# Hybrid decoder layer on one core: short products alternated with long ones in a planned order, and norm weights that ride with x

## The chip, the cores and the metric

The kernel runs on one core of a Trainium2 chip. The metric is the device time of one execution in microseconds. Five engines carry it: TensorE (PE; its weight loads are listed apart, as PEld), VectorE (DVE), ScalarE (ACT), GpSimd (POOL), and SyncE (SP), which here only starts DMAs.

## What is computed

One layer of a decoder for 512 tokens of width 1024, all in fp32. Cut to what matters here:

```
h = rmsnorm(x, norm_mix_g)
c_q, c_kv, k_r, u_ssm, x_q, gate_logits = split(h @ w_in)
y_a = mla_branch(...) @ w_o_mla        # 8 heads, causal attention in blocks of 128
y_b = s5_branch(u_ssm, ...) @ w_o_ssm  # 32 groups, state 64, complex diagonal scan, GLU
y_c = cross_branch(x_q, mem, ...) @ w_o_cross  # 4 heads over 256 memory tokens
x = x + (sum_i sigmoid(gate_i) * y_i) @ w_out
up = causal_dwconv(rmsnorm(x, norm_ffn_g) @ w_up, conv_w, conv_b)   # width 3, 2 x 2816 columns
x = x + (silu(up_g) * up_v) @ w_down
```

In the S5 branch the coefficients of the state space model are worked out on the chip from lambda, dt, B and C. The cross branch multiplies the normed memory by w_mem_kv (1024 x 1024).

## The kernel before

**Products.** Every large fp32 product is three products of a faster type (fp32r). `split` (L456) makes a high part of an operand on ACT and the rest, the low part, by a subtraction on DVE or POOL; `mm3` (L489) multiplies high by high, high by low and low by high into the same PSUM bank. The stationary operand of a product is at most 128 columns, the moving one mostly 512. Weights come in units of 128 x 1024: `wload` (L471) starts the DMA on SP into one of two slots "wr", `wsplit` (L479) makes the two parts in one of three slots "ws". A unit of w_in or w_out feeds 24 products of 512 columns. A unit of w_mem_kv feeds 12 (two chunks of the contraction, two token tiles, three products).

**Short products.** Beside the long ones PE runs transposes (128 x 128, results in `pstr`), products with 128 moving columns (in `pssc`), the statistics (stationary `accx` or `am`, moving a single column `ones`), and, for the state space model, products of 32 and 96 columns with stationary `pad` tiles that have 32 columns (shown as `128*32`).

**What sets the order.** `trace` (L413) runs the kernel once as a draft, in which each instruction becomes an Op. The text ORDER (L54) has one letter for each step of a generator: h is `gen_xstats`, m `gen_mem`, a `gen_stage_a`, s, p, t and e the state space model, and so on; the last stages, `w_out_ffn` (L1312), come behind all of them. `order_ops` (L263) then lists the Ops for five engines at once: it takes the Op that could start first by a table of costs (`_lengths`, L159), adds a lag (LAG) before other engines may use a result, lets some Ops choose between DVE, ACT and POOL, and does so twice, the second time with urgencies from the first. The engines' instructions are issued in that order by one line, L1464, so that every row of the profile has this line and is told by its tiles. On each engine the order is fixed: an instruction that waits holds back all behind it on its engine.

**The start.** Eleven matmuls on a zero tile (`wz`) run while the first DMAs are under way. For each of the eight chunks of x, SP starts the chunk `xc` and its weights `wu`; behind the first chunk SP also starts a small DMA for `pg`, the norm weights of x, and POOL's queue one for `pv`, all other per-column parameters. ACT and DVE make `xs` (high and low) from `xc` and `pg`, and 12 products for each chunk give the input of the state space model. `acc` (`accx` in rows) collects the squares of x.

**The statistics.** `gen_xstats` (L562) sums `accx` over partitions by eight products with one moving column. Four of them read a contiguous stationary block of 128 columns, four every fourth column (`acc[:, t::4]`). DVE copies the sums to `mx`, POOL raises them to the power -0.5, four transposes of `mx` spread the result over partitions, and a copy to `rB` on DVE ends it. Meanwhile and after that DVE works through the state space coefficients: small operations on `ang`, `ap`, `den`, `pw`, then wide ones on `Bp`, `bt` and `G`, between the low parts of weight units.

**The end.** The down projection makes eight tiles of the output. The last one (m = 7) is made in two halves of 256 columns, 66 products each, each with its own add on DVE and its DMA on SP.

Of the kernel before, what the change touches and what calls it, by code (L numbers as in the profile page):

```python
# [18 lines left out]
KC = D // 128  # L19
# [19 lines left out]
def _split_bits(v, bits):  # L39
# [15 lines left out]
    "aZmsemhha1pupakpp1pttktmt2utpt11ppxpepxtupxtttctp1cxxuttYtatkd1taxggdxgg1dcxaccrdBcccdddBd1qdBBdqdqq2dvvvwvwCq"  # L55
    "vwvq2wqvv00v2wCvwwvwvwvwvvwwqww0w2q2wwvqwwwvqvvv0wwvvvq0qw2wqwCv0wvvvww0wvwwwvwvwvwww0v2wwwCAAAA"
# [7 lines left out]
PSUM_TAGS = ("mm", "sc", "tr")  # L64
LAG = {"PE": 2000.0, "V": 600.0, "S": 600.0, "P": 600.0, "SP": 60.0}
# [8 lines left out]
class Op:  # L74
    __slots__ = ("eng", "calls", "var", "idx", "touch", "deps", "succ", "nbytes", "tiles", "step", "acc")
# [61 lines left out]
def describe(op, tiles):  # L137
# [18 lines left out]
    op.acc = "PE" in op.calls  # L156


def _lengths(op, eng, nm, args, kw, outs, ins, tiles):  # L159
# [12 lines left out]
    if eng == "PE":  # L172
        st, mov = (ins[1], ins[0]) if nm == "transpose" else (ins[0], ins[1])
        if nm == "transpose":
            n, p = _free(st), _free(mov)
            ldw = p / 1.2 + 5
            return max(n / 2.4 + 2, ldw), 275.0, ldw, lock, func
        n, p = _free(mov), _free(st)
        ldw = (p / 1.2 + 5) * (2 if st.ap[-1][0] > 1 else 1)
        if mov.dtype == F32:  # L180
            half = max(n / 1.2 + 4, ldw)
            return 2 * half, n / 1.2 + half + 175, ldw, lock, func
        return max(13 + n / 2.4, ldw), n / 2.4 + 176, ldw, lock, func
# [79 lines left out]
def order_ops(ops, bufs, urgency=None):  # L263
# [23 lines left out]
    dma_free, dve_busy, pool_busy = 0.0, (0.0, 0.0), (0.0, 0.0)  # L287
# [41 lines left out]
    while done < len(ops):  # L329
        best = None  # L330
        for e in engs:
            a, pick, rk = avail[e], None, ranks[e]
            for i in cand[e]:
                op = ops[i]
                r = max(ready_at[i][e], a)
                if (best is not None and r >= best[0]) or (pick is not None and (r, rk[i]) > pick[:2]):
                    continue
# [34 lines left out]
        else:  # L372
# [40 lines left out]
def trace(alloc, V, S, P, T, SP, VP, VS, VSP, xT, memT, pos, freq, pv, grow, lam, sbc, dcol, wu, wa, wqb, wkvb, wglu, wxk, wxq, wmem,  # L413
# [84 lines left out]
    for _ in range(11):  # L498
# [3 lines left out]
    pvt, pg = cst([128, NPV], b="pv"), cst([128, KC], b="pg")  # L502
# [23 lines left out]
    ur = [k8([128, 4, L], b="wu") for _ in range(2)]  # L526
    for kc in range(KC):
        xcs.append(k2([128, L], b="xc"))
        SP.dma_start(xcs[kc], xT[:, kc])
        if kc == 0:  # L530

            SP.dma_start(pg, pv[:, PV["norm_mix_g"]:PV["norm_mix_g"] + KC])
            P.dma_start(pvt, pv)
        SP.dma_start(ur[kc // 4][:, kc % 4], wu[:, kc])
    for kc in range(KC):
# [776 lines left out]
    def w_out_ffn():  # L1312
# [58 lines left out]
        for m in range(KC):  # L1371
            p = ps("mm")
            halves = [slice(0, L)] if m < KC - 1 else [slice(0, 256), slice(256, L)]
# [115 lines left out]
def _layout(inp):  # L1489
# [5 lines left out]
    o["xT"] = _rows(np.ascontiguousarray(w["x"].T))  # L1495
    o["memT"] = _rows(np.ascontiguousarray(w["mem"].T))
# [66 lines left out]
```

## Time and profile before

| | before |
|---|---|
| time, median of 3 runs | 847.66 us (847.46 to 848.22) |
| profiled execution | 848.97 us |
| its span | 847.2 us |
| PE busy | 839.4 us, 4284 instructions |
| DVE busy | 593.2 us, 1092 instructions |
| ACT busy | 387.5 us, 658 instructions |
| POOL busy | 110.9 us, 118 instructions |
| DMA | 81.03 MB, mean 96 GB/s |

The span is what the hardware profiler records of one execution from the first to the last instruction. Starts and durations in rows are in us from the start of the span; an "x4" at a row's end joins four instructions in a row, and then the duration runs from the first start to the last end. Records of products overlap, since they are pipelined: the pitch of a product is the time from its start to the start of the next one.

### The profile page before, as it was taken

Reading aid. Unit: us, or ns where it says so; the run is one execution under the profiler, and the core shown is the slowest. Engines: PE = TensorE matmul, PEld = TensorE weight load, DVE = VectorE, ACT = ScalarE, POOL = GpSimd, SP = SyncE. Lnnn points to the kernel's source line nnn. Section 1 sums busy time; section 2 is a strip of 40 time slices with the busy share of each in tenths; the row PEclk is TensorE's granted clock in tenths of the full one; section 3 lists DMA queues with packets and bytes.
Section 4 is the critical chain, followed back from the end, with each engine's and each line's share of the span. In section 5 each row is a group of like instructions: output and inputs, shape, how many; then the busy total and the mean of one; then the engine's idle time right before and its main releaser. Section 6 shows DMA issues by size and latency. Waiting matters only on the chain.

```text
span 847.2 us, 11358 instructions
## 1 busy us (share of the span) xinstructions
PE 839.4 (99%) x4284; PEld 718.3 (85%) x4284; DVE 593.2 (70%) x1092; ACT 387.5 (46%) x658; POOL 110.9 (13%) x118
## 2 busy tenths in 40 slices
PE   9999999999999999999999999999999999999997
PEld 9878899998888888888888888888888888888887
DVE  7989998997677788768686539777777777423221
ACT  7746345547534575656444336444444444212110
POOL 5573141002112122120000002000000000000000
PEclk9899999999999999999999999999999999999999
DMA  9323322113123212321433323333333222333330
GB/s 320 118 77 98 117 64 75 51 59 104 44 72 88 88 40 69 118 75 51 149 124 100 100 75 99 100 100 100 99 100 97 91 90 90 118 111 106 119 100 26
DMA packets 26055, 81.03 MB, mean 96 GB/s; under 512 B 3104, under 2 KB 3664, under 8 KB 26000
## 3 DMA queue, kind: packets, MB, share of 16 engines
q1 hardware_dynamic: 25632, 79.45, 28.9%
q0 software_dynamic: 368, 0.85, 0.3%
q8 instruction: 34, 0.56, 0.3%
q14 instruction: 21, 0.17, 0.1%
HBM read 78.19 MB, written 2.10 MB: 95 GB/s over the span
## 4 chain that ended last, share of the span: by engine, by line
PE 93%; DVE 2%; DMA 2%; ACT 1%; issue 1%; POOL 1%; SPq 0%; DVEq 0%; POOLq 0%; ACTq 0%
PE psmm L1464 83%; PE pssc L1464 6%; PE pstr L1464 5%; DMA xc<-in_xT_dram 1%; DMA wr<-in_wg_dram 1%; POOL am L1464 0%; DVE ws L1464 0%; SPq L1464 0%; ACT ws L1464 0%; DVE ang L1464 0%; DVE ms L1464 0%; ACT xs L1464 0%; DVE am L1464 0%; DVE accx L1464 0%; POOL pad L1464 0%
## 5 line engine op out<-in xcount | busy, mean ns | idle before, releaser
L1464 ACT ACTIVATE ws<-wr 128x1024 fp32r<-128x1024 f32 (+3 forms) x140 | 142.7, 1021 | 322.0 <-PE psmm L1464 270.7
L1464 PE MATMUL psmm<-hs,ws 128*128 128x512 f32 x1008 | 229.4, 389 | 0.0
L1464 DVE TENSOR_TENSOR ws<-wr,ws 128x1024 fp32r<-128x1024 f32 x135 | 161.6, 1198 | 87.0 <-ACT ws L1464 86.6
L1464 PEld LDWEIGHTS psmm<-hs,ws 128*128 128x128 f32 x1008 | 189.0, 188 | 39.2
L1464 PE MATMUL psmm<-xs,ws 128*128 128x512 f32 x696 | 172.0, 396 | 0.0
L1464 PEld LDWEIGHTS psmm<-xs,ws 128*128 128x128 f32 x696 | 127.3, 188 | 25.2
L1464 PE MATMUL psmm<-act,ws 128*128 128x512 f32 (+1 forms) x594 | 120.7, 365 | 0.0
L1464 PEld LDWEIGHTS psmm<-act,ws 128*128 128x128 f32 x594 | 102.7, 189 | 18.1
L1464 DVE SCALAR_TENSOR_TENSOR cv<-z,pv,cv 128x511 f32<-128x511 f32 (+1 forms) x88 | 67.2, 770 | 1.0 <-ACT cv L1464 0.3
L1464 DVE TENSOR_TENSOR z<-psmm,r2B 128x512 f32<-128x512 f32 x42 | 29.0, 690 | 47.5 <-PE psmm L1464 47.5
L1464 PE MATMUL psmm<-mrg,ws 128*128 128x512 f32 x192 | 43.7, 389 | 0.0
L1464 PEld LDWEIGHTS psmm<-mrg,ws 128*128 128x128 f32 x192 | 36.0, 188 | 7.5
L1464 PE MATMUL psmm<-ws,xs 128*128 128x288 f32 (+2 forms) x240 | 39.8, 314 | 0.0
L1464 PEld LDWEIGHTS psmm<-ws,xs 128*128 128x128 f32 x240 | 36.9, 214 | 0.3
L1464 ACT ACTIVATE cv<-z,pv 128x512 f32<-128x512 f32 x44 | 35.0, 800 | 0.3 <-DVE z L1464 0.3
L1464 PE MATMUL psmm<-ws,ms 128*128 128x512 f32 x96 | 25.6, 426 | 0.0
L1464 DVE SCALAR_TENSOR_TENSOR gt<-gt,psmm 128x512 f32<-128x512 f32 x24 | 16.2, 683 | 12.9 <-PE psmm L1464 12.9
L1464 DVE TENSOR_TENSOR gt<-psmm,rB 128x512 f32<-128x512 f32 x24 | 16.3, 683 | 12.4 <-PE psmm L1464 12.1
L1464 PE MATMUL psmm<-xo,ws 128*128 128x512 f32 x96 | 24.7, 398 | 0.0
L1464 DVE TENSOR_TENSOR o<-psmm,x 128x512 f32<-128x512 f32 (+1 forms) x9 | 5.6, 631 | 26.3 <-PE psmm L1464 26.3
L1464 ACT ACTIVATE e<-pssc,nms,qsc 128x128 f32<-128x128 f32 (+3 forms) x32 | 19.6, 615 | 7.9 <-DVE nms L1464 7.6
L1464 PEld LDWEIGHTS psmm<-ws,ms 128*128 128x128 f32 x96 | 19.6, 209 | 4.3
(299 smaller groups left out, 1154.1 us busy)
## 6 DMA issues: line engine op xcount, KB each, us to landing
wr<-in_wup_dram SPq DMA_DIRECT2D x44, 512.0 KB, 3.5
wr<-in_wg_dram SPq DMA_DIRECT2D x24, 512.0 KB, 3.4
wr<-in_wdn_dram SPq DMA_DIRECT2D x16, 512.0 KB, 3.5
wr<-in_wmem_dram SPq DMA_DIRECT2D x8, 512.0 KB, 3.6
wr<-in_wout_dram SPq DMA_DIRECT2D x8, 512.0 KB, 3.5
wr<-in_wdn_dram SPq DMA_DIRECT2D x8, 384.0 KB, 3.0
wr<-in_wa_dram SPq DMA_DIRECT2D x5, 512.0 KB, 4.1
xc<-in_xT_dram SPq DMA_DIRECT2D x8, 256.0 KB, 6.3
```

What stands on the lines that cost most here:

```text
L1464: getattr(issue[ops[i].eng], name)(*args, **kw)
```

## The change

The scheduler, for products on PE: a product whose weight load is longer than its stream is now marked `short`. A transpose takes 35 ns of PE in the table instead of at least its weight load, and the other products are no longer held to at least their weight load. Instead a short product may only start `BETWEEN` = 225 ns or more after the last short one ended, so that the list puts long products between. ORDER is a new text of the same length. Then, in the program: the first chunk of x carries the eight columns of norm weights (input `xg`, tile `x0`), the DMA for `pg` is gone, and that for `pv` goes to SP behind the third chunk; the warm-up has 9 matmuls instead of 11; `gen_xstats` first copies `acc` with its columns rearranged to `accp`, so that the last four statistics read contiguous blocks; and the last output tile is made by 66 products of 512 columns, with its two adds as before and the second DMA on ACT's queue.

```diff
 ORDER = (
-    "aZmsemhha1pupakpp1pttktmt2utpt11ppxpepxtupxtttctp1cxxuttYtatkd1taxggdxgg1dcxaccrdBcccdddBd1qdBBdqdqq2dvvvwvwCq"
+    "Zesaphmhpeutmtppmtppp1ptu1xtx1aptp1xptu2kuttattpt1ttaxktcYxacxat1gkgcgxgdxc1drccd1BddccBdddBdqBqddq2vqvwvvvwww"
...
+BETWEEN = 225.0
...
+    op.short = op.acc and op.var["PE"][3] > 0
...
     if eng == "PE":
         st, mov = (ins[1], ins[0]) if nm == "transpose" else (ins[0], ins[1])
         if nm == "transpose":
-            n, p = _free(st), _free(mov)
-            ldw = p / 1.2 + 5
-            return max(n / 2.4 + 2, ldw), 275.0, ldw, lock, func
+            ldw = _free(mov) / 1.2 + 5
+            return 35.0, 275.0, ldw, max(ldw - 35.0, 0.0), func
...
-        return max(13 + n / 2.4, ldw), n / 2.4 + 176, ldw, lock, func
+        return 13 + n / 2.4, n / 2.4 + 176, ldw, max(ldw - 13 - n / 2.4, 0.0), func
...
                 r = max(ready_at[i][e], a)
+                if op.short:
+                    r = max(r, short_end + BETWEEN)
...
+            if op.short:
+                t = max(t, short_end + lock)
+                short_end = t + occ
...
-    for _ in range(11):
+    for _ in range(9):
         T.matmul(pz[:, :128], wz, wz, start=True, stop=True)
...
+    x0 = k8([128, L + KC], b="x0")
+    pg = x0[:, L:]
     for kc in range(KC):
-        xcs.append(k2([128, L], b="xc"))
-        SP.dma_start(xcs[kc], xT[:, kc])
-        if kc == 0:
-
-            SP.dma_start(pg, pv[:, PV["norm_mix_g"]:PV["norm_mix_g"] + KC])
-            P.dma_start(pvt, pv)
+        xcs.append(x0[:, :L] if kc == 0 else k2([128, L], b="xc"))
+        SP.dma_start(x0 if kc == 0 else xcs[kc], xg if kc == 0 else xT[:, kc])
         SP.dma_start(ur[kc // 4][:, kc % 4], wu[:, kc])
+        if kc == 2:
+            SP.dma_start(pvt, pv)
...
     def gen_xstats():
+        ap4 = k2([128, 4, 128], b="accp")
+        VS.tensor_copy(ap4, acc.rearrange("p (j t) -> p t j", t=4))
         pm = ps("tr")
         for t in range(4):
             T.matmul(pm[:, t:t + 1], acc[:, t * 128:(t + 1) * 128], ones, start=True, stop=True)
-            T.matmul(pm[:, 4 + t:5 + t], acc[:, t::4], ones, start=True, stop=True)
+        for t in range(4):
+            T.matmul(pm[:, 4 + t:5 + t], ap4[:, t], ones, start=True, stop=True)
...
-            halves = [slice(0, L)] if m < KC - 1 else [slice(0, 256), slice(256, L)]
...
-            for c in halves:
-                for k in range(NFF):
-                    u = un[k // 8]
-                    sl = slice((k % 8) * 128, (k % 8) * 128 + 128)
-                    mm3(p[:, c], u[:, 0, sl], u[:, 1, sl], act[0][k][:, c], act[1][k][:, c], k == 0, k == NFF - 1)
+            for k in range(NFF):
+                u = un[k // 8]
+                sl = slice((k % 8) * 128, (k % 8) * 128 + 128)
+                mm3(p, u[:, 0, sl], u[:, 1, sl], act[0][k], act[1][k], k == 0, k == NFF - 1)
...
-                SP.dma_start(outT[m, :, c], o[:, c])
+                (S if c.start else SP).dma_start(outT[m, :, c], o[:, c])
```

The order shows the rest. First PE at the first of four groups of products with `pad` (32 and 96 moving columns). Before, most of them run behind one another, here the last of the group:

```order
L1464 MATMUL pstr_250<-pad_152_234,pad_230 32x32
L1464 MATMUL pstr_250<-pad_153_235,pad_231 32x32
L1464 MATMUL pstr_250<-pad_232,pad_230 32x96
L1464 MATMUL pstr_250<-pad_233,pad_231 32x96
L1464 MATMUL psmm_258<-xs_90,ws_260 128x512
```

Now, the first of the same group:

```order
L1476 MATMUL psmm_252<-ws_261,ms_198 128x512
L1476 MATMUL pstr_244<-pad_103_185,pad_181 32x32
L1476 MATMUL psmm_253<-ws_261,ms_194 128x512
L1476 MATMUL pstr_244<-pad_104_186,pad_182 32x32
L1476 MATMUL pstr_244<-pad_183,pad_181 32x96
L1476 MATMUL psmm_253<-ws_261,ms_198 128x512
```

A product of 512 columns now stands between the two of 32 columns, and one behind that of 96; in the whole program the products with 32 stationary columns stand in 18 runs instead of 5. The other short products (transposes, and those with 128 columns), 476 in both programs, stand in 338 runs instead of 82.

The second place is PE at the first four transposes of `pad`. In `psmm`, products of `ws` with `ms` belong to a unit of w_mem_kv, products of `xs` with `ws` to a unit of w_in. Before, the units of w_mem_kv that stood behind the statistics were done by then, and two units of w_in were open:

```order
L1464 MATMUL psmm_222<-xs_97,ws_224 128x512
L1464 MATMUL psmm_226<-xs_90,ws_228 128x512
L1464 MATMUL psmm_226<-xs_98,ws_228 128x512
L1464 MATMUL psmm_242<-xs_90,ws_244 128x512
L1464 MATMUL psmm_242<-xs_98,ws_244 128x512
L1464 MATMUL pstr_240<-idt_88,pad_230 128x128 x4
L1464 MATMUL psmm_226<-xs_90,ws_228 128x512
```

Now (`ws_255`, `ws_257`, `ws_259` and `ws_261` are the last four of the eight units of w_mem_kv):

```order
L1476 MATMUL psmm_253<-ws_255,ms_195 128x512
L1476 MATMUL psmm_252<-ws_257,ms_192 128x512
L1476 MATMUL psmm_253<-ws_257,ms_192 128x512
L1476 MATMUL pstr_214<-idt_87,pad_181 128x128
L1476 MATMUL psmm_252<-ws_257,ms_192 128x512
L1476 MATMUL pstr_214<-idt_87,pad_181 128x128
L1476 MATMUL psmm_252<-ws_257,ms_196 128x512
L1476 MATMUL pstr_214<-idt_87,pad_181 128x128
L1476 MATMUL psmm_253<-ws_257,ms_192 128x512
```

All eight units of w_mem_kv, 12 products each, now follow the statistics at once. Before, only the four of the first half did, the fourth of them mixed with a unit of w_in, and then came units of w_in with 24 products each. From the statistics to the first use of the low part of `ws_261`, the last unit, PE now has 86 products of 512 columns, 16 transposes and three or four products of 128 columns, among them the rows shown here.

DVE over the same stretch. Before:

```order
L1464 TENSOR_TENSOR G_200<-bt_198,ap_168 128x1024
L1464 TENSOR_TENSOR ws_218<-wr_217,ws_218 128x1024
L1464 TENSOR_TENSOR ws_224<-wr_223,ws_224 128x1024
L1464 TENSOR_TENSOR Bp_199<-Bp_199,bt_198 128x16x16 x2
L1464 TENSOR_TENSOR G_200<-bt_198,ap_168 128x1024
```

Now:

```order
L1476 TENSOR_TENSOR ws_257<-wr_256,ws_257 128x1024
L1476 TENSOR_TENSOR ws_259<-wr_258,ws_259 128x1024
L1476 TENSOR_TENSOR Bp_162<-Bp_162,bt_161 128x16x48
L1476 TENSOR_TENSOR bt_161<-bt_161,ap_150 128x1024
L1476 TENSOR_TENSOR G_163<-bt_161,ap_150 128x1024
L1476 TENSOR_TENSOR G_163<-G_163,bt_161 128x1024
L1476 TENSOR_TENSOR bt_161<-bt_161,ap_150 128x1024
L1476 TENSOR_TENSOR ws_261<-wr_260,ws_261 128x1024
```

The same wide operations on Bp, bt and G are there, but nearly all of them stand between the statistics' `mx` and the low part of the last unit of w_mem_kv (`ws_261`), with the low parts of four other such units among them.

## Rows read from the trace of the kernel before

**Rows 1.** The page: busy time of the engines, and the chain of work that ended last, by engine.

```profile
PE 839.4 (99%) x4284; PEld 718.3 (85%) x4284; DVE 593.2 (70%) x1092; ACT 387.5 (46%) x658; POOL 110.9 (13%) x118
...
PE 93%; DVE 2%; DMA 2%; ACT 1%; issue 1%; POOL 1%; SPq 0%; DVEq 0%; POOLq 0%; ACTq 0%
```

**Rows 2.** What PE waited for in the whole span: us in total, times, the longest (two more rows, the last, have 1.0 us at the start and 0.4).

```profile
PE pstr L1464 <- POOL pad L1464: 1.9, 1, 1.9
```

**Rows 3.** Engines by stretch, the stretch right behind the statistics: us, then busy time of PE, PEld, DVE, ACT and POOL with instructions, the clock granted to PE as a share of full speed, DMA share and GB/s.

```profile
37.90:43.60 5.70, 5.70 (x15) 4.45 (x16) 2.97 (x19) 3.97 (x8) 1.65 (x1) 0.50 0.26 94
```

**Rows 4.** The timeline of PE around the statistics: start, duration, tiles.

```profile
34.03 1.43 PE L1464 MATMUL pstr<-ones,accx 128*128 128x1 f32 x8
...
37.90 6.99 PE L1464 MATMUL psmm<-ws,ms 128*128 128x512 f32 x18
44.72 0.60 PE L1464 MATMUL pstr<-idt,mx 128*128 128x128 f32 x4
```

**Rows 5.** The timeline of DVE behind the statistics: start, duration, tiles.

```profile
38.80 0.16 DVE L1464 TENSOR_SCALAR mx<-pstr 128x8 f32<-128x8 f32 x1
...
40.74 0.18 DVE L1464 TENSOR_TENSOR ap<-ang 128x16 f32<-128x16 f32 x1
45.36 0.69 DVE L1464 COPY rB<-pstr 128x512 f32<-128x512 f32 x1 [4.43 <-PE pstr L1464]
...
46.90 0.68 DVE L1464 TENSOR_TENSOR Bp<-bt,ang 128x512 f32<-128x512 f32 x1
...
48.10 1.21 DVE L1464 TENSOR_TENSOR G<-bt,ap 128x1024 f32<-128x1024 f32 x1
49.24 2.35 DVE L1464 TENSOR_TENSOR ws<-wr,ws 128x1024 fp32r<-128x1024 f32 x2
51.51 0.75 DVE L1464 TENSOR_TENSOR Bp<-Bp,bt 128x256 f32<-128x256 f32 x2
...
53.32 0.95 DVE L1464 TENSOR_TENSOR Bp<-Bp,ap 128x768 f32<-128x768 f32 x1
54.19 0.95 DVE L1464 TENSOR_TENSOR bt<-Bp,ap 128x768 f32<-128x768 f32 x1
...
56.91 1.69 DVE L1464 TENSOR_TENSOR bt<-Bp,ap 128x768 f32<-128x768 f32 x1
58.52 3.39 DVE L1464 TENSOR_TENSOR ws<-wr,ws 128x1024 fp32r<-128x1024 f32 x2
61.83 1.79 DVE L1464 TENSOR_TENSOR Bp<-Bp,bt 128x768 f32<-128x768 f32 x1
63.66 2.20 DVE L1464 TENSOR_TENSOR bt<-bt,ap 128x1024 f32<-128x1024 f32 x1
```

**Rows 6.** The timeline of POOL over the same time.

```profile
39.03 1.65 POOL L1464 TENSOR_TENSOR mx<-mx,mhalf 128x8 f32<-128x8 f32 x1 [1.57 <-DVE mx L1464]
...
57.74 1.74 POOL L1464 TENSOR_TENSOR sqkx<-kx 128x512 f32<-128x512 f32 x1
59.55 1.28 POOL L1464 COPY pad<-Bp 64x256 f32<-64x256 f32 x1
```

**Rows 7.** The timeline of PE at two transposes that stand alone between products of 512 columns (the third row is that of a narrower stretch and leaves the first two of the seven products out).

```profile
256.23 0.27 PE L1464 MATMUL pstr<-idt,qf 128*128 128x128 f32 x1
256.26 1.87 PE L1464 MATMUL psmm<-xs,ws 128*128 128x512 f32 x7
...
256.81 1.32 PE L1464 MATMUL psmm<-xs,ws 128*128 128x512 f32 x5
...
257.96 0.27 PE L1464 MATMUL pstr<-idt,qf 128*128 128x128 f32 x1
```

**Rows 8.** The timeline of PE at four transposes in a row.

```profile
379.13 1.52 PE L1464 MATMUL psmm<-xs,ws 128*128 128x512 f32 x6
380.50 0.60 PE L1464 MATMUL pstr<-idt,kh 128*128 128x128 f32 x4
380.85 0.71 PE L1464 MATMUL psmm<-xs,ws 128*128 128x512 f32 x2
381.40 0.33 PE L1464 MATMUL pssc<-qk,qk 128*128 128x128 f32 x2
```

**Rows 9.** The timeline of PE at a run of 32 products with `pad` between products of 512 columns, in narrow stretches: the last product ahead of it, its first five, its last four, the two products behind it.

```profile
100.58 0.40 PE L1464 MATMUL psmm<-xs,ws 128*128 128x512 f32 x1
100.91 0.40 PE L1464 MATMUL pstr<-pad,pad 128*32 128x32 f32 x5
...
102.43 0.50 PE L1464 MATMUL pstr<-pad,pad 128*32 128x96 f32 x4
102.85 0.50 PE L1464 MATMUL psmm<-xs,ws 128*128 128x512 f32 x1
...
103.19 0.40 PE L1464 MATMUL psmm<-xs,ws 128*128 128x512 f32 x1
```

**Rows 10.** The end: the last output tile's products on PE, and the two adds on DVE.

```profile
826.79 15.99 PE L1464 MATMUL psmm<-act,ws 128*128 128x256 f32 x132
...
842.82 0.76 DVE L1464 TENSOR_TENSOR o<-psmm,x 128x256 f32<-128x256 f32 x2 [13.99 <-PE psmm L1464]
```

**Rows 11.** The start: the high part of the first chunk of x on ACT, and PE's first product.

```profile
4.97 0.72 ACT L1464 ACTIVATE xs<-xc,pg 128x512 fp32r<-128x512 f32 x1
...
5.76 1.33 PE L1464 MATMUL psmm<-ws,xs 128*128 128x512 f32 x4
```

More of the change, by code (lines that the diff above doesn't have):

```diff
@@ L54 @@
 ORDER = (
-    "aZmsemhha1pupakpp1pttktmt2utpt11ppxpepxtupxtttctp1cxxuttYtatkd1taxggdxgg1dcxaccrdBcccdddBd1qdBBdqdqq2dvvvwvwCq"
-    "vwvq2wqvv00v2wCvwwvwvwvwvvwwqww0w2q2wwvqwwwvqvvv0wwvvvq0qw2wqwCv0wvvvww0wvwwwvwvwvwww0v2wwwCAAAA"
+    "Zesaphmhpeutmtppmtppp1ptu1xtx1aptp1xptu2kuttattpt1ttaxktcYxacxat1gkgcgxgdxc1drccd1BddccBdddBdqBqddq2vqvwvvvwww"
+    "dv2qwqwv2CqwvvwwvCv0wwvvqwv2wwqwvv2wqwwCqvvwqvwqv2vvwwwqw0vvw0vvw0w0vv2wwwwwwwvvvwvw0www00CwAAAA"
 )
@@ L74 @@
 class Op:
-    __slots__ = ("eng", "calls", "var", "idx", "touch", "deps", "succ", "nbytes", "tiles", "step", "acc")
+    __slots__ = ("eng", "calls", "var", "idx", "touch", "deps", "succ", "nbytes", "tiles", "step", "acc", "short")
 class Program(list):
@@ L180, in _lengths @@
         if mov.dtype == F32:
-            half = max(n / 1.2 + 4, ldw)
-            return 2 * half, n / 1.2 + half + 175, ldw, lock, func
-        return max(13 + n / 2.4, ldw), n / 2.4 + 176, ldw, lock, func
+            half, one = max(n / 1.2 + 4, ldw), max(n / 2.4 + 4, 30)
+            return one + half, n / 1.2 + half + 175, ldw, max(ldw - one, 0.0), func
+        return 13 + n / 2.4, n / 2.4 + 176, ldw, max(ldw - 13 - n / 2.4, 0.0), func
     if eng == "V":
@@ L286, in order_ops @@
     start = [0.0] * len(ops)
-    dma_free, dve_busy, pool_busy = 0.0, (0.0, 0.0), (0.0, 0.0)
+    dma_free, dve_busy, pool_busy, short_end = 0.0, (0.0, 0.0), (0.0, 0.0), -1e9
     table = None
@@ L410, in order_ops, with trace @@
     return sorted(range(len(ops)), key=lambda i: (start[i], i)), start
-def trace(alloc, V, S, P, T, SP, VP, VS, VSP, xT, memT, pos, freq, pv, grow, lam, sbc, dcol, wu, wa, wqb, wkvb, wglu, wxk, wxq, wmem,
+def trace(alloc, V, S, P, T, SP, VP, VS, VSP, xT, xg, memT, pos, freq, pv, grow, lam, sbc, dcol, wu, wa, wqb, wkvb, wglu, wxk, wxq, wmem,
           wg, woa, wob, woc, wout, wup, wdn, outT):
@@ L497, in trace @@
     pz = ps("tr")
-    for _ in range(11):
+    for _ in range(9):
         T.matmul(pz[:, :128], wz, wz, start=True, stop=True)
-    pvt, pg = cst([128, NPV], b="pv"), cst([128, KC], b="pg")
+    pvt = cst([128, NPV], b="pv")
     def pc(name, i=0):
@@ L1376, in w_out_ffn @@
                 un.append(wunit(wdn[m, :, k0 * 128:(k0 + kn) * 128], kn * 128))
-            for c in halves:
-                for k in range(NFF):
-                    u = un[k // 8]
-                    sl = slice((k % 8) * 128, (k % 8) * 128 + 128)
-                    mm3(p[:, c], u[:, 0, sl], u[:, 1, sl], act[0][k][:, c], act[1][k][:, c], k == 0, k == NFF - 1)
+            for k in range(NFF):
+                u = un[k // 8]
+                sl = slice((k % 8) * 128, (k % 8) * 128 + 128)
+                mm3(p, u[:, 0, sl], u[:, 1, sl], act[0][k], act[1][k], k == 0, k == NFF - 1)
             o = k2([128, L], b="o")
-            for c in halves:
+            for c in [slice(0, L)] if m < KC - 1 else [slice(0, 256), slice(256, L)]:
                 add(o[:, c], p[:, c], x1[m][:, c])
-                SP.dma_start(outT[m, :, c], o[:, c])
+                (S if c.start else SP).dma_start(outT[m, :, c], o[:, c])
     def once(*fs):
@@ L1495, in _layout @@
     o["xT"] = _rows(np.ascontiguousarray(w["x"].T))
+    o["xg"] = np.ascontiguousarray(np.concatenate([o["xT"][:, 0], _cols(w["norm_mix_g"])], 1))
     o["memT"] = _rows(np.ascontiguousarray(w["mem"].T))
```

## The prediction

> **What bounds the kernel now.** I read the page first, for which engine is full and which carries the chain: PE is busy 99% of the span and is 93% of the chain [rows 1]. Then the waits of PE, for what a new order could take away: three, and only one over 1.0 us [rows 2]. So the time is the sum of PE's pitches, and the only ways to gain are fewer or denser pitches, or the few waits. Then I read pitches, as start to start in the timeline of PE. Six products of 512 columns take 380.50 - 379.13 = 1.37 us, 0.228 each [rows 8]. From 379.13 to 381.40 stand eight of them and four transposes: 2.27 - 8 x 0.228 = 0.45, so 0.11 us for a transpose in a row of such. That is about four times the 0.03 us by which the next product's record starts behind a transpose that stands alone (256.26 behind 256.23 [rows 7]): the stream is short, and what is paid is a weight load. This is what the change is after.
>
> **Does alternating pay?** The trace already has transposes alone between products of 512 columns. From 256.23 to 256.81 are one transpose and two products; the five products from 256.81 to 257.96 have 1.15 / 5 = 0.230 each, so the transpose costs 0.58 - 0.46 = 0.12 us [rows 7]. That is no less than in a row (0.11). The product behind it starts early, but the one behind that is late by as much: the pitch is the longer of a product's stream and the weight load of what follows, whoever stands beside whom. So 256 more separate runs (338 against 82) save nothing, and at 0 to 0.01 us more for each (0.12 against 0.11) they cost 0 to 2.6 us; I take 0.005 each, **+1.3**.
>
> **Products with pad.** Here standing apart costs. In the run of 32 the last product ahead starts at 100.58 and the first short one at 100.91: 0.33 instead of 0.23. The last four start 0.25 / 3 = 0.083 apart, but from 102.68, where the last of them starts, to the next product at 102.85 it is 0.17, and that product's own pitch is 103.19 - 102.85 = 0.34 [rows 9]. So 0.10 to enter, 0.09 to leave and 0.11 for the product behind: 0.30 us for each run, whatever its length. With 18 runs instead of 5 that is 13 x 0.30 = **+4.0**. Were only the last part paid again (the short ones' small loads could hide), it would be 13 x 0.11 = 1.4; these are the bounds. The page "TensorEngine Tiling (Array Packing)" of the Trainium skill (Tiling Modes, Key Properties) has a rule that speaks against this change: "Changing tiling mode (not just tile) drains the TensorE". The rows with 128*128 and 128*32 tiles side by side agree with it in direction; it gives no figure.
>
> **What is removed.** (a) Statistics: from 34.03 to 37.90 are 20 instructions in 3.87 us [rows 4]; at a weight load each they would take 20 x 0.11 = 2.2. The contiguous copy and the new place of the memory's sums, behind the others, should give that: **-1.6** (bounds -1.0 to -1.9). The copy itself is one more operation of 128x512 on DVE or ACT, about 0.7 us like `rB` [rows 5], while PE has products in hand. (b) The clock granted to PE right behind the statistics is 0.50, the lower of its two levels, for 5.7 us [rows 3], after PE had run those 3.87 us of single columns: 18 products take 44.72 - 37.90 = 6.82 instead of 4.10 us [rows 4]. With half as long a run of such instructions it should stay up: **-2.7** (it may not, 1 in 3). (c) The one long wait, transposes of `pad` for POOL [rows 2], stands elsewhere: **-1.9**, and what comes in its place is counted below. (d) The last tile: 132 products of 256 columns take 842.82 - 826.79 = 16.0 us with some 0.3 of latency, 0.119 each; 66 of 512 columns take 66 x 0.228 = 15.0: **-0.7**. Both adds stood behind the last product before too [rows 10], so the tail stays, with one DMA on another queue at nothing. (e) The start: the first product follows the high part of x, which ACT makes at 4.97 behind a square of x and a weight part [rows 11]; now it comes first, and the norm weights need no DMA of their own: **-0.3** (0 to -0.8). `pv` moves from POOL's queue to SP behind the third chunk; the five chunks behind it come a little later, its first users are the memory's parts much later; nothing. Two warm-ups less lie ahead of the first product anyway.
>
> **What is added: DVE between the statistics and the last unit of w_mem_kv.** A unit of w_in gives PE 24 products, 5.5 us, for one low part of 1.14 us on DVE; a unit of w_mem_kv only 12, 2.7 us. All eight now stand together, exactly where DVE has the wide coefficient operations. PE's work from the statistics to the first use of the last unit's low part is 86 x 0.228 + 20 x 0.112 = 21.8 us. DVE's over the same stretch, by starts in [rows 5]: `mx` to `ap` 2.1; `rB` and the small ones behind it to the first `Bp` 1.5; `Bp` and `bt` to `G` 1.2; five low parts at 2.27 / 2 = 1.14, 5.7; five operations of 1024 columns at 1.14 (as `G`), 5.7; the two short `Bp` 0.7; six of 768 columns at 0.87, 5.2. Sum 22.1 us, if nothing disturbs. But where POOL works beside it [rows 6] the same operations take longer: the `bt` at 56.91 1.6 instead of 0.87, the two low parts at 58.52 3.3 instead of 2.3, the `Bp` at 61.83 1.8 instead of 0.87 [rows 5], together +2.7. And `rB` needs `mx` raised on POOL, 1.65 us, and four transposes that now stand between products, some 1.4 us more, while DVE has only 2.1 us of other work: about +1.5. So 26.3 against 21.8: PE waits 4.5. `mx` itself started 0.9 behind the statistics [rows 4, 5], behind a low part; now a low part, an operation on `cq` and a small one stand ahead of it: +1.2 (0 to 2.5). What is queued behind the waiting product is all of PE's later work, so the wait is paid in full: **+6** (2 without POOL's disturbance and with DVE on time, 10 with all wide operations slowed by half).
>
> The clock of (b) does not come on top: whether PE is slow or fast there, DVE's queue ends when it ends, and a lower clock only eats the wait. If the wait itself brings the clock down, up to 2.7 us are added, as behind the statistics now.
>
> **Sum.** -1.6 - 2.7 - 1.9 - 0.7 - 0.3 = -7.2; +4.0 + 1.3 + 6 = +11.3; together +4.1 us. Against the profiled execution's span of 847.2 that is 851.3; its own time is 848.97, 1.3 above the median of the runs, 847.66, and a median stands about 0.5 above such a span. So **851.8 us**.
>
> **The rivals.** (1) DVE keeps up. POOL's copies fall elsewhere, `mx` is on time, and the wait is 0 to 1 us. Then -7.2 + 5.3 + 0.5 gives 846.3, the same; with the pad runs at their lower bound and no cost for single transposes, -7.2 + 1.4 + 0.5 = -5.3, 842.4, faster. This is the case on the other side: its place is DVE's queue from `mx` to the last low part, and with the pad runs at 1.4 it decides for faster as soon as the wait is under about 2.8 us. For it: 22.1 us undisturbed is only 0.3 more than PE's 21.8. Against it: rows at 56.91 to 63.66 are disturbed one after the other. (2) Alternating does pay, by hiding the short ones' weight loads wholly. Then each of 338 runs saves about 0.08 us (0.11 less the 0.03 of its stream): 27 us together, and -7.2 + 4.0 - 27 + 6 = -24 gives about 824. Against it stand the two transposes in [rows 7], which are exactly this case. The page "TensorE: Matmul & The Clock Gate" of the Trainium skill (Step-by-step) speaks for it: weight loads are pulled ahead of products in flight when they go to the background weight buffer. In the trace one load is ahead, not two. (3) The wait is longer, 9 to 12 us, since the last unit's weights and the coefficients' transposes wait in turn: 855 to 858. (4) The order does nothing at all beyond the small edits, with the wait at 2.5 to 3.5: 848 to 849.
>
> **How the numbers follow.** A measurement of this kernel can tell about 0.2%, 1.7 us, from no change. The forecast (wait 4 to 9, 849.4 to 855) has 0.50, rival 3 0.08, both slower: 0.58. Same: rival 4 and the middle of rival 1, 0.20. Faster: rival 1 with cheap pad runs 0.17, rival 2 0.05: 0.22. The range leaves out rival 2, the best of rival 1 and the worst of rival 3: 843.5 to 856.
>
> **What would show it.** A wait of PE on DVE's `ws` or `pad` some 15 to 25 us behind the statistics, of 4 to 9 us: right; none over 1 us: the main step is wrong. The pitch of a product behind a pad product 0.34 with 0.33 ahead of it: the 4.0 is right. Single transposes that cost clearly under 0.11 us: rival 2, and then all of the sum is wrong. The statistics in about 2.2 us and a clock of 1.00 behind them: (a) and (b). The last tile in 15.0 us: (d).

## The result

The changed kernel takes 859.11 us in the median of four runs (857.12 to 860.38), the kernel before 847.56 beside it (845.64 to 848.22). These two medians are 11.6 us apart; the ratio on record, which the table of experiments uses too, is 1.0124, with an interval of 1.0103 to 1.0145, and so slower by some 10.5 us. The profiled execution has a span of 857.9 us against 847.2. I had forecast slower, but 4.1 us, and the time lies above the range of 843.5 to 856.

The page of the changed kernel, busy times and the chain, to be held against [rows 1]:

```profile
PE 843.9 (98%) x4214; PEld 709.7 (83%) x4214; DVE 589.6 (69%) x1091; ACT 385.7 (45%) x656; POOL 108.9 (13%) x118
...
PE 91%; DVE 5%; issue 2%; DMA 1%; ACT 1%; SPq 0%; DVEq 0%
```

PE is busy 4.5 us longer with 70 instructions fewer, and VectorE holds 5% of the chain instead of 2%: both kinds of loss are there, denser work lost and waits. The waits of PE (us in total, times, the longest), where [rows 2] had one for `pad`:

```profile
PE psmm L1476 <- DVE cq L1476: 3.3, 1, 3.3
PE pstr L1476 <- ACT pad L1476: 2.0, 1, 2.0
PE psmm L1476 <- DVE ws L1476: 1.4, 2, 0.8
...
PE pstr L1476 <- DVE e L1476: 0.7, 1, 0.7
PE psmm L1476 <- ACT ws L1476: 0.6, 1, 0.6
PE pssc L1476 <- ACT e L1476: 0.5, 1, 0.5
```

The place behind the statistics, the timeline of PE (start, duration, tiles), against [rows 4]:

```profile
34.03 0.95 PE L1476 MATMUL pstr<-ones,accx 128*128 128x1 f32 x8
34.84 1.03 PE L1476 MATMUL pstr<-ones,accp 128*128 128x1 f32 x8
35.73 0.58 PE L1476 MATMUL pstr<-ones,am 128*128 128x1 f32 x4
39.61 5.06 PE L1476 MATMUL psmm<-ws,ms 128*128 128x512 f32 x11 [3.29 <-DVE cq L1476]
...
45.09 0.28 PE L1476 MATMUL pstr<-idt,mx 128*128 128x128 f32 x1
45.12 0.48 PE L1476 MATMUL psmm<-ws,ms 128*128 128x512 f32 x1
45.44 0.27 PE L1476 MATMUL pstr<-idt,mx 128*128 128x128 f32 x1
...
45.81 11.14 PE L1476 MATMUL psmm<-ws,ms 128*128 128x512 f32 x48
58.99 0.33 PE L1476 MATMUL pstr<-idt,pad 128*128 128x128 f32 x1 [2.04 <-ACT pad L1476]
59.92 0.50 PE L1476 MATMUL psmm<-ws,ms 128*128 128x512 f32 x1 [0.60 <-DVE ws L1476]
...
68.46 0.50 PE L1476 MATMUL psmm<-ws,ms 128*128 128x512 f32 x1 [0.82 <-DVE ws L1476]
```

The statistics, all 20 instructions, now take 2.2 us, 34.03 to about 36.2, instead of 3.87. Then PE stands still for 3.3 us, until VectorE has read a PSUM bank (`cq`) that the next product needs. And a transpose that stands alone, from 45.09 to 45.44 with its one product, costs 0.35 - 0.23 = 0.12 us, as in [rows 7]. VectorE over the same time, against [rows 5], and POOL at its beginning:

```profile
35.08 1.78 DVE L1476 TENSOR_SCALAR ang<-ang 128x80 f32<-128x80 f32 x1
...
36.90 0.20 DVE L1476 TENSOR_SCALAR ang<-ang 128x80 f32<-128x80 f32 x1
...
37.57 1.22 DVE L1476 TENSOR_TENSOR ws<-wr,ws 128x1024 fp32r<-128x1024 f32 x1
...
38.81 0.74 DVE L1476 SCALAR_TENSOR_TENSOR cq<-psmm,pv,cq 128x512 fp32r<-128x512 f32 x1
39.47 0.15 DVE L1476 TENSOR_SCALAR mx<-pstr 128x8 f32<-128x8 f32 x1
...
46.09 0.69 DVE L1476 COPY rB<-pstr 128x512 f32<-128x512 f32 x1 [4.57 <-PE pstr L1476]
...
66.99 1.42 DVE L1476 TENSOR_TENSOR ws<-wr,ws 128x1024 fp32r<-128x1024 f32 x1
```

```profile
35.35 1.46 POOL L1476 MEMSET pad<- 128x512 f32 x3
```

`mx` starts 3.3 us behind the statistics (0.9 before), and then VectorE itself is idle for 4.6 us until PE has run the transposes behind `rB`: PE runs the products ahead of them late and at the lower clock. The clock, by stretch, in the columns of [rows 3]:

```profile
38.00:44.00 6.00, 4.39 (x10) 3.47 (x11) 3.49 (x23) 2.94 (x7) 2.37 (x2) 0.52 0.24 87
```

To see where the whole difference lies, I added up, over all products of PE behind the warm-up, the time from start to start less the pitch that each has where nothing disturbs it (0.228 us for 512 columns, 0.174 for 384, 0.13 for 288, 0.120 for 256, 0.11 for a short one, 0.032 and 0.083 for the pad ones). What is left over, in us:

| up to, us | before | changed | difference in the stretch |
|---|---|---|---|
| 34 | 6.7 | 6.7 | 0 |
| 38 | 8.4 | 6.7 | -1.7 |
| 70 | 13.3 | 17.5 | +5.9 |
| 110 | 14.3 | 21.2 | +2.7 |
| 260 | 15.4 | 24.0 | +1.7 |
| 310 | 15.7 | 26.9 | +2.6 |
| the end | 15.0 | 26.5 | +0.3 |

The sum is +11.5; less 0.8 for the last tile (82 products of 512 columns up to its add, 834.82 to 853.60 with some 0.3 of latency, so 0.226 each, against 0.119 for half of one in [rows 10]) that is the 10.7 between the spans.

### The profile page after: what moved, and what is told of

It is laid out like the page before. It is cut to its first block, busy times and chain, and to the rows that moved or that the text cites. A ratio compares the mean times of both kernels' runs of the same rounds, so it can differ in the third digit from the quotient of the medians.

```text
span 857.9 us, 11228 instructions
## 1 busy us (share of the span) xinstructions
PE 843.9 (98%) x4214; PEld 709.7 (83%) x4214; DVE 589.6 (69%) x1091; ACT 385.7 (45%) x656; POOL 108.9 (13%) x118
## 4 chain that ended last, share of the span: by engine, by line
PE 91%; DVE 5%; issue 2%; DMA 1%; ACT 1%; SPq 0%; DVEq 0%
PE psmm L1476 81%; PE pssc L1476 5%; PE pstr L1476 5%; DVE ws L1476 1%; DMA xc<-in_xT_dram 1%; DVE Bp L1476 0%; DVE ang L1476 0%; DVE ms L1476 0%; DVE G L1476 0%; DVE xs L1476 0%; SPq L1476 0%; ACT ws L1476 0%; DVE bt L1476 0%; DVE accx L1476 0%; ACT e L1476 0%
## 5 line engine op out<-in xcount | busy, mean ns | idle before, releaser
L1476 ACT ACTIVATE ws<-wr 128x1024 fp32r<-128x1024 f32 (+2 forms) x140 | 142.8, 1020 | 316.2 <-PE psmm L1476 271.9
L1476 DVE TENSOR_TENSOR ws<-wr,ws 128x1024 fp32r<-128x1024 f32 (+1 forms) x137 | 165.9, 1212 | 89.7 <-ACT ws L1476 89.5
L1476 PE MATMUL psmm<-xs,ws 128*128 128x512 f32 x696 | 193.1, 416 | 0.0
L1476 PE MATMUL psmm<-act,ws 128*128 128x512 f32 x528 | 119.8, 389 | 0.0
L1476 PEld LDWEIGHTS psmm<-act,ws 128*128 128x128 f32 x528 | 99.1, 188 | 20.6
L1476 PE MATMUL psmm<-ws,xs 128*128 128x288 f32 (+2 forms) x240 | 45.3, 326 | 0.6 <-ACT ws L1476 0.6
L1476 PE MATMUL psmm<-ws,ms 128*128 128x512 f32 x96 | 29.2, 447 | 4.7 <-DVE cq L1476 3.3
L1476 PE MATMUL pstr<-idt,e 128*128 128x128 f32 x112 | 29.6, 272 | 0.7 <-DVE e L1476 0.7
L1476 DVE SCALAR_TENSOR_TENSOR gt<-gt,psmm 128x512 f32<-128x512 f32 x24 | 16.3, 682 | 15.7 <-PE psmm L1476 15.7
L1476 ACT ACTIVATE PT<-pstr 128x128 fp32r<-128x128 f32 (+3 forms) x32 | 14.0, 437 | 23.6 <-PE pstr L1476 23.4
L1476 PE MATMUL pssc<-qk,qk 128*128 128x128 f32 (+3 forms) x96 | 23.5, 333 | 0.5 <-ACT e L1476 0.5
```

The costliest lines, as they stand in the source:

```text
L1476: getattr(issue[ops[i].eng], name)(*args, **kw)
```

## The experiments

My theory: the pad runs and the single transposes cost what their pitches say (about 5 us), and the rest is an order of instructions in which VectorE and PE wait for each other behind the statistics. The rivals: alternation as such makes the loss; the new ORDER text makes it; VectorE's total work makes it, whatever its order; the clock makes nothing on top.

All ratios are to the kernel before on the same chip; the changed kernel's own, 1.0124, stands for 857.9 us of span. The span is that of one profiled execution.

| run | ratio (interval) | span, us |
|---|---|---|
| small_edits | 1.0022 (1.0012 to 1.0032) | 848.7 |
| old_order | 1.0322 (1.0303 to 1.0341) | 873.4 |
| old_sched | 1.0124 (1.0093 to 1.0155) | 856.5 |
| early_mx | 1.0108 (1.0085 to 1.0130) | 855.0 |
| fill | 1.0110 (1.0094 to 1.0125) | 854.9 |
| whole_pads | 1.0087 (1.0072 to 1.0102) | 855.5 |
| whole_t | 1.0096 (1.0081 to 1.0110) | 854.6 |
| combo | 1.0068 (1.0051 to 1.0084) | 850.0 |
| half_coef | 1.0087 (1.0067 to 1.0106) | 854.6 |
| half_combo | 1.0027 (1.0017 to 1.0038) | 848.8 |
| soft | 1.0034 (1.0019 to 1.0049) | 848.7 |
| hand_stats | 1.0011 (1.0000 to 1.0022) | 848.9 |
| hand_stats_tile | 1.0006 (0.9993 to 1.0018) | 845.9 |

**The parts of the change.** Three kernels take it apart. *small_edits* is the kernel before, its ORDER, `_lengths` and `order_ops` included, with the edits to the program alone, of which these are the cores:

```diff
+    x0 = k8([128, L + KC], b="x0")
...
+        VS.tensor_copy(ap4, acc.rearrange("p (j t) -> p t j", t=4))
...
+                mm3(p, u[:, 0, sl], u[:, 1, sl], act[0][k], act[1][k], k == 0, k == NFF - 1)
```

> The kernel before with the small edits alone (x0 with the norm weights, pv on SP, 9 warm-ups, contiguous statistics, last tile in one); scheduler rules and ORDER as before. My theory: the small edits gain, 1.7 us at the statistics and 0.7 at the last tile, nothing at the start; 844 to 846 us. Rival (a small edit, such as pv on SP or the extra copy, is what made the changed kernel slow): 850 us or more.

It is 0.2% slower than before, so the theory was wrong on the sign, and the rival's 850 us is nearly reached, though this is a sixth of what the changed kernel loses. The greedy list shifts with any edit: here PE waits 1.2 us for `xs` at 21.98, which it did not before, and the transposes of `mx` come directly behind the statistics, so that PE waits for POOL.

```profile
40.91 1.11 PE L1470 MATMUL pstr<-idt,mx 128*128 128x128 f32 x4 [2.96 <-POOL mx L1470]
```

The 1.7 us won at the statistics are a wait of 3.0 us a moment later. *old_order* has the new scheduler rules with the old text:

```diff
 ORDER = (
-    "Zesaphmhpeutmtppmtppp1ptu1xtx1aptp1xptu2kuttattpt1ttaxktcYxacxat1gkgcgxgdxc1drccd1BddccBdddBdqBqddq2vqvwvvvwww"
+    "aZmsemhha1pupakpp1pttktmt2utpt11ppxpepxtupxtttctp1cxxuttYtatkd1taxggdxgg1dcxaccrdBcccdddBd1qdBBdqdqq2dvvvwvwCq"
```

> The changed kernel with the ORDER text of before: alternation without the new text. My theory: broken pad runs cost some 4 us and single transposes about 1, less 2.4 from the small edits; with no crowd of memory units behind the statistics 849 to 852 us. Rival (the new text is all of the loss): 844 to 846 us. Second rival (alternation makes all of the loss): 856 us or more.

At 1.0322 it is far worse than either kernel and than my theory. By its number alone the second rival, that alternation makes all of the loss, would hold, but *old_sched* below speaks against that. What the trace shows is a list full of waits. The three longest:

```profile
PE psmm L1476 <- DVE vv L1476: 4.6, 1, 4.6
PE psmm L1476 <- DVE cq L1476: 2.7, 2, 2.2
PE pssc L1476 <- DVE z L1476: 2.3, 1, 2.3
```

*old_sched* has the new text with the old rules (`_lengths`, `order_ops` and `Op` of before; no `short`, no `BETWEEN`).

> The changed kernel with the scheduler rules of before, so the new ORDER text without alternation. My theory: VectorE's queue behind the statistics stays late (5 to 6 us), the pad runs are whole: 850 to 854 us. Rival (alternation makes all of the loss): 844 to 846 us.

Without any alternation it is as slow as the changed kernel, by other waits, and so my theory missed here too:

```profile
PE pstr L1470 <- POOL mx L1470: 2.5, 1, 2.5
PE psmm L1470 <- DVE qf L1470: 2.2, 1, 2.2
PE psmm L1470 <- DVE nk L1470: 2.0, 3, 0.9
```

So neither text nor rules can be priced by swapping them: every swap draws the whole order anew, and its waits are as large as the effect. From here on I moved single instructions in the finished list and left all others where they were.

**VectorE's order behind the statistics.** In *early_mx*, `defer(order, ops, late, until)` puts the instructions `late`, and what depends on them, behind the last of `until`:

```diff
+    v = [i for i in order if ops[i].eng == "V"]
+    m = next(n for n, i in enumerate(v) if named(ops[i], "mx"))
+    c = max(n for n in range(m) if named(ops[v[n]], "cq"))
+    s = max(n for n in range(c) if named(ops[v[n]], "ms"))
+    order = defer(order, ops, v[s + 1:c], [v[m + 1]])
+    return defer(order, ops, [v[c]], [v[m]])
...
     order, _ = order_ops(ops, bufs, latest(ops, start))
+    order = early_mx(order, ops)
```

> The changed kernel with three VectorE instructions moved: the first step of mx and the low part of cq stand ahead of the operations on ang and of a low part of ws, right behind the statistics. Nothing else moves. My theory (the loss behind the statistics starts from VectorE reaching cq and mx 3.3 us late): TensorE's wait for cq falls from 3.3 to about 1 us, rB comes 3 to 6 us earlier, and the gain is carried to the end: 3.5 us (5.5 if the clock stays up), so 853.5 to 855.5 us. Rival (VectorE's total work up to the last memory unit sets the time, whatever its order): the waits move to the later places, 858 to 859 us.

```profile
37.25 4.33 PE L1509 MATMUL psmm<-ws,ms 128*128 128x512 f32 x11 [0.87 <-DVE cq L1509]
...
55.10 0.33 PE L1509 MATMUL pstr<-idt,pad 128*128 128x128 f32 x1 [1.49 <-ACT pad L1509]
56.58 0.50 PE L1509 MATMUL psmm<-ws,ms 128*128 128x512 f32 x1 [1.15 <-DVE ws L1509]
```

The wait for `cq` is 0.9, the first product 2.4 us and the first transpose of `pad` 3.9 us earlier than in the changed kernel, where three instructions moved. That is more than the first wait, since `rB` came 3.3 us earlier too (42.75 by VectorE's timeline). In the span 2.9 us are left, by the ratios 1.4, which the intervals don't part from none: behind the second pair of waits the clock fell again (the products from 57.63 on stand 0.45 apart). The median, 856.6 us, lies between what theory and rival expected. The rival, that the waits merely move, is out at this place.

**The clock.** *fill* gives PE work in the gap, behind the last product of the statistics (`last`), and takes nothing else away:

```diff
             getattr(issue[ops[i].eng], name)(*args, **kw)
+            if i == KEEP["last"]:
+                for _ in range(15):
+                    nc.tensor.matmul(KEEP["pm"][:, 128:], KEEP["x"][:, :128], KEEP["x"][:, 128:], start=True, stop=True)
```

> The changed kernel with 15 products of 384 columns added right behind the statistics, into the 3.3 us in which TensorE waits for cq; their results go to unused columns of the statistics' bank and are not read. My theory: TensorE does not go idle there, the granted clock stays at 1.00 if the 2 us of statistics alone don't bring it down, the 14 products ahead of rB no longer lose 2.6 us, rB comes that much earlier on VectorE and the whole gain is kept: 2.6 us, 856 to 857 us. Rival (as my prediction had it: the lower clock only eats into waits that VectorE's queue makes anyway): the waits for pad and ws grow by the same amount, 858.5 to 859.5 us.

Two stretches behind the statistics, and one behind the later waits, in the columns of [rows 3]:

```profile
38.00:39.00 1.00, 1.00 (x7) 1.00 (x7) 0.50 (x3) 0.15 (x2) 0.59 (x1) 1.00 0.55 106
39.00:40.00 1.00, 1.00 (x6) 0.80 (x5) 0.94 (x11) 0.00 (x0) 1.00 (x1) 1.00 0.81 311
...
57.00:58.00 1.00, 1.00 (x5) 0.65 (x3) 1.00 (x2) 0.00 (x0) 0.00 (x0) 0.50 0.60 115
```

And PE behind the added products, and VectorE's operation on `cq`:

```profile
38.86 2.70 PE L1478 MATMUL psmm<-ws,ms 128*128 128x512 f32 x11
41.40 0.27 PE L1478 MATMUL pstr<-idt,mx 128*128 128x128 f32 x1
...
37.51 0.74 DVE L1478 SCALAR_TENSOR_TENSOR cq<-psmm,pv,cq 128x512 fp32r<-128x512 f32 x1
```

With dense products in the gap the clock stays at 1.00 behind the statistics, the first transpose of `mx` starts at 41.40 instead of 44.47, and the first of `pad` at 55.64 instead of 58.99. Of the 3.1 us at the first transpose 2.3 are the clock: the eleven products ahead of it take 2.54 us instead of 4.86. The rest is chance: the operation on `ang` that took 1.78 us in the changed kernel took 0.38 here, so that `cq` and `mx` came 1.3 us earlier and the first of these products 0.75. The waits for `pad` and `ws` do not grow (2.0 and 0.6, as in the changed kernel): the lower clock had not been eating into them. Then the clock fell once more, behind those waits, and took a part back; by the ratios 1.2 us are left of 3, which their intervals don't part from none, and the median, 858.05, lies between theory and rival. What decides between them is the trace.

**The pad runs.** *whole_pads* puts each group's 32 products (`g`) together:

```diff
+    for g in groups.values():
+        inside = order[order.index(g[0]) + 1:order.index(g[-1])]
+        order = defer(order, ops, [i for i in inside if ops[i].eng == "PE" and i not in g], g)
```

> The changed kernel with the 32 products with 32 stationary columns of each of the four groups kept together (4 runs instead of 18), by putting the products between them behind them; nothing else moves. My theory: each run costs 0.30 us to enter and leave, so 14 x 0.30 = 4.2 us less, 854 to 855.5 us. Rival (the lower bound, only the product behind a run is held up): 1.5 us less, 857 to 858.

PE's busy time falls from 843.9 to 840.0 us (the page), 3.9 / 14 = 0.28 for each run that is gone; counted from the first product with 32 stationary columns on, it is 783.0 against 778.8, 0.30 for each, as read in [rows 9]. The lower bound is out. The rule of the page "TensorEngine Tiling (Array Packing)" of the Trainium skill (Tiling Modes, Key Properties), that a change of tiling mode drains the engine, agrees with this number. In the first group 1.6 us came back as a wait for a copy that the split order had hidden:

```profile
PE pstr L1511 <- DVE pad L1511: 1.6, 1, 1.6
```

By the ratios some 3 us are gained.

**The single short products.** *whole_t* does the same with those of one PSUM tile that stand at most three instructions apart (`runs`), 109 runs instead of 338:

```diff
+        for r in runs:
+            inside = order[order.index(r[0]) + 1:order.index(r[-1])]
+            order = defer(order, ops, [i for i in inside if ops[i].eng == "PE" and i not in r], r)
```

> The changed kernel with the short products of one PSUM tile (transposes, products of 128 columns) that stand at most three instructions apart put together again: 109 runs instead of 338, nothing else changed. My theory: a transpose costs 0.12 us alone and 0.11 in a row, so about 229 x 0.005 = 1.2 us less (0 to 2.3), 857 to 859 us. Rival (alternating hides weight loads): clearly slower, by up to 229 x 0.08 = 18 us.

PE's busy time falls by 1.2 us (842.7), which is the forecast's figure, but only by luck. Ahead of the first product with 32 stationary columns (at 69.34 us, and at 66.34 here) it falls by 0.8, and there PE worked at the lower clock for 3.4 us instead of 5.4. Behind that place it is 783.0 and 782.5 us, so 0.5 us for nearly all of the 229, 0.002 each. The rival that weight loads are hidden between long products is out for these shapes: the time went down, not up by 18 us. The page "TensorE: Matmul & The Clock Gate" of the Trainium skill (Step-by-step) speaks for that rival, with weight loads pulled ahead of products in flight. The span fell by more (3.3), since the transposes behind `rB`, now four in a row, the shorter stretch at the lower clock, and a `cq` that happened to come 1.3 us earlier (the operation on `ang` took 0.38 us here too) let VectorE start sooner:

```profile
38.35 4.38 PE L1523 MATMUL psmm<-ws,ms 128*128 128x512 f32 x11 [2.27 <-DVE cq L1523]
42.56 0.60 PE L1523 MATMUL pstr<-idt,mx 128*128 128x128 f32 x4
```

*combo* has the three moves at once.

> The changed kernel with all three moves: early cq and mx, whole pad groups, shorts together again. My theory: the parts lie at different places and add up: 2.9 (measured in the span of the first) + 4.2 + 1.2, so about 851 us (849 to 853). Rival (they compete for the same waits, so that denser products only wait longer for VectorE): 854 us or more.

The profiled execution is as forecast (851.8 us, span 850.0). The median is not: at 854.13 (1.0068, so 5.8 us above before) it lies above the range and in the rival's, since the three other runs took 1.9 to 2.9 us longer, at a mean clock of 0.996 instead of 0.997. That the parts add up is shown by one execution only.

**VectorE's load.** *half_coef* takes work away up to the last memory unit without leaving any out (580 is the copy of the last pad of group 1; 697, 698 and 700 are put behind it with the second halves):

```diff
+    order = defer(order, ops, [697, 698, 700], [580])
+    rest = []
...
+            if ops[i].eng == "V" and name == "tensor_tensor" and len(args[0].shape) == 4 and tuple(args[0].shape)[1::2] == (GP, 16):
+                rest.append((name, tuple(x[:, 8:] for x in args), kw))
+                args = tuple(x[:, :8] for x in args)
             getattr(issue[ops[i].eng], name)(*args, **kw)
+            if i == 580:
+                for name, args, kw in rest:
+                    getattr(nc.vector, name)(*args, **kw)
```

> The changed kernel with the twelve wide operations on Bp, bt and G split: each is done for its first half (groups of state 0 and 1) at its old place, the second halves stand together behind the low part of the unit after the last memory unit, where the first reader of the second half (pad of group 2) is put too. VectorE has about 5 us less to do up to the last memory unit's low part. My theory (VectorE's queue from rB to that low part sets the time): the waits of TensorE for pad and ws between 56 and 68 us (2.0, 0.6, 0.8, and the latency with them 4.0) vanish nearly whole, the wait for cq stays: 3 to 4 us less, 855 to 856. Rival (ACT's copies of pad, or weights, set those waits): less than 1 us, 858 to 859.

```profile
PE psmm L1503 <- DVE cq L1503: 3.3, 1, 3.3
PE pstr L1503 <- ACT pad L1503: 1.5, 1, 1.5
PE pstr L1503 <- DVE ones L1503: 1.0, 1, 1.0
```

Both waits for `ws` are gone; by the span 3.3 us are gained, by the ratios 3.1. Some 0.7 of this is not the halves: `rB` itself starts at 45.36 instead of 46.09, since the lower clock ended 1.6 us earlier here. VectorE's queue did set the waits for `ws`. The wait for `pad` did not vanish, it is 1.5 instead of 2.0, and here the rival has a share. In the changed kernel ACT has the high part of a unit, which waits 1.0 us for its DMA, ahead of the copies of `pad`:

```profile
57.17 1.06 ACT L1476 ACTIVATE ws<-wr 128x1024 fp32r<-128x1024 f32 x1 [0.99 <-DMA wr<-in_wmem_dram]
58.14 0.80 ACT L1476 COPY pad<-Bp 64x256 f32<-64x256 f32 x2
```

*half_combo* joins the halves to the three moves.

> The same with all three moves of the run before: early cq and mx, whole pad groups, shorts together. My theory: what is left of the change behind the statistics goes too, some 4 us below the run with the three moves: 848.5 to 850.5 us, or 0.1 to 0.4% above the kernel before; the rest is the wait in the softmax at 272 us. Rival: 852 us or more.

At 1.0027, 2.3 us above before, nearly the whole loss is undone with text and rules of the change, by moving instructions and by cutting twelve operations in two. The remaining waits lie elsewhere; one of them is a softmax at 270 to 285 us that had none before. There ACT, in the changed kernel, has the high part of a weight unit ahead of an exponential, and that part waits 2.1 us for its slot:

```profile
277.83 1.06 ACT L1476 ACTIVATE ws<-wr 128x1024 fp32r<-128x1024 f32 x1 [2.08 <-issue]
278.80 0.55 ACT L1476 ACTIVATE e<-pssc,nms,qsc 128x256 f32<-128x256 f32 x1
```

*soft* is *half_combo* with that exponential ahead of the unit on ACT, and its reciprocal and product ahead of the unit's low part on VectorE.

> The run with halved coefficients and the three moves, and one more place: at 272 us a softmax exponential on ACT now stands ahead of the high part of a weight unit that waits for a free slot, and on VectorE its reciprocal and product stand ahead of that unit's low part. My theory (the last 2.4 us over the kernel before are this softmax queued behind a weight unit): TensorE's waits for e (0.7 and 0.5 us, with the pitches around them 1.8) shrink to about 0.5, 1.2 us less: 849 to 850 us. Rival (the softmax needs its own time anyway, or the unit's low part is then late): no change, 850.5 to 851 us.

No change. The first wait (0.7) vanished, the second, for the next exponential, grew from 0.5 to 1.1.

```profile
273.28 1.55 PE L1555 MATMUL pssc<-qk,qk 128*128 128x384 f32 x6 [1.06 <-ACT e L1555]
```

So what this place costs is not just that order; its cause stays open.

**What the kernel before could gain.** *hand_stats* leaves its order untouched and makes only the statistics contiguous (ACT copies into the tile of `rB`):

```diff
+            if i in odd:
+                args = (args[0], accp[:, odd[i]], args[2])
             getattr(issue[ops[i].eng], name)(*args, **kw)
+            if i == copy_at:
+                getattr(issue["S"], "copy")(accp, KEEP["acc"].rearrange("p (j t) -> p t j", t=4))
```

> The kernel before, its order untouched, with the contiguous statistics alone: ACT copies the squares rearranged into the tile of rB, which is free then, and four of the statistics read that. My theory: the statistics take 1.6 us less; whether the granted clock still falls behind them is open, 2.7 us more if it does not: 843.3 us if it stays up, 846 if it falls. Rival (the time goes into a wait for mx, as in the run with the small edits): 847 to 848 us.

```profile
37.65 0.61 PE L1473 MATMUL pstr<-ones,am 128*128 128x1 f32 x4 [1.79 <-POOL am L1473]
```

Nothing is gained (849.16 against 848.33 us), so the rival was right, though at another place than it named: the first eight products end in front of the memory's sums, which POOL has not finished (before, PE waited 0.4 us for them). *hand_stats_tile* adds the last tile in one.

> The same with the last output tile in one group of 66 products of 512 columns instead of 132 of 256. My theory: 0.7 us less than the run with the statistics alone. Rival: no difference (within 0.3 us), since the last add waits for the last product in both.

The two differ by 0.05%, less than their intervals, so the 0.8 us read in the pitches can't be told from none by the times. No version that I ran beats the kernel before.

## Why the prediction was right in sign and wrong in size

| term | forecast, us | measured, us |
|---|---|---|
| statistics | -1.6 | -1.7, but PE then waits |
| clock behind them | -2.7 | -2.7, but it fell again: 2.6 of the +10.5 below |
| wait for `pad` of before | -1.9 | -1.9 |
| last tile | -0.7 | -0.8 |
| start | -0.3 | 0: first product at 5.33 instead of 5.76, statistics at 34.03 in both |
| pad runs | +4.0 | 13 x 0.30 = +3.9 |
| single shorts | +1.3 | 256 x 0.002 = +0.5 |
| from the statistics to the last memory unit | +6 | +10.5 |
| softmax at 270 to 285 us | not named | +2.6 |

The right column adds up to +10.4, with 10.7 between the spans. The 2.6 of the clock are 14 products and four transposes that took 45.81 - 39.61 = 6.20 us instead of 14 x 0.228 + 4 x 0.11 = 3.6.

**The step that failed** is the one on VectorE behind the statistics, in two of its terms and in the sentence on the clock. PE used the low part of the last memory unit at 68.46, 32.3 us behind the statistics' end at 36.2; PE's own work there is 21.8, so it was 10.5 late and not 6. The main term held in sum: from `rB` at 46.09 to the end of that low part at 68.41 VectorE took 22.3 us, forecast 20.0 + 2.7. Where the 2.7 came from is in part luck: of the operations that the prediction named, the `bt` and the `Bp` of 768 columns were not slowed (0.96 and 0.95 us), and low parts were (two in 3.20 us at 49.06 and two in 2.75 at 58.45, instead of 2.35 [rows 5]).

Two terms were mis-sized. `mx` came 3.3 us behind the statistics, and the sum had counted 1.2 (with the 0.9 of before, the prediction's own words give 2.1). An operation on `ang` of 0.20 us took 1.78 while POOL ran its memsets; in *fill* and *whole_t* it took 0.38 at the same place, so this part differs between executions. And `cq`, for which PE waited, I had not counted as a wait at all.

The other term is the wait of VectorE for `rB`, 4.6 instead of 1.5. Of these 3.1 us 2.6 are the clock, as worked out above: I wrote that a lower clock "only eats the wait", as if VectorE ran by itself. It does not. `rB` needs four transposes that stand behind eleven products on PE, and those started late, after the gap, and took 0.43 us each instead of 0.228. Slow PE, late `rB`, late VectorE, waiting PE: a loop, in which a gap is paid twice, as a wait and as slow products behind it. *fill* showed it (2.3 us at the first of these transposes), *early_mx* showed where it begins, and *half_coef* that VectorE's queue carries it on.

**Right** were the steps from pitches. A transpose cost 0.11 us in a row and 0.12 alone; the price of single shorts had the right sign but came out at 0.5 us instead of 1.3. A run with 32 stationary columns cost 0.28 to 0.30 us to enter and leave. Rival 1, that VectorE keeps up, and rival 2, that alternation pays, are out; rival 3, the wait of 9 to 12 us, is what came, though for another reason than the one given.

**Not foreseen** were 2.6 us in a softmax. I had looked for the first place at which the new order crowds an engine and not gone on to the next.

## What to carry to other kernels

Where two engines feed each other, an estimate must follow the loop: an engine's lateness is not only the sum of its own queue, but also what it waits for from the engine that waits for it. Alternating short products with long ones was worth nothing here, where a transpose takes 0.11 us in a row and 0.12 alone; read one lone short product in the trace before planning for it. When PE's busy time changes by about 1 us, look whether the stretches at the lower clock are as long in both traces. And a list made by a greedy planner is redrawn by any edit, so that an effect of 0.5% is tested by moving instructions in the finished list, not by changing the planner.

## What the runs showed of the hardware

The granted clock differs between runs of one kernel, and most of the spread of its times goes with it. Of 68 timed runs of the kernel before, 15 had a mean clock of 0.999 or 1.000 and a median of 846.4 us, 38 had 0.997 or 0.998 and 848.2, 15 had less and 849.6: 1.8 and 1.4 us from one group to the next. In the changed kernel the clock fell to 0.50 at 38.2 us, in the gap of 3.3 us behind 2.2 us of statistics; with the gap filled it did not fall there, but behind a pair of waits 18 us later. With a gap of 0.9 us it fell in the traces of *early_mx* and *half_combo* and not in those of *combo* and *soft*, which these runs don't explain.
